# Ten groups of a decoder trunk: the load two weights ahead goes behind the adding transfer, the squares of the next weights behind the keys' last square

## The chip, the core and the metric

The kernel runs on one core of a Trainium2 chip. The metric is the device time of one execution in microseconds (us); three timed runs of the kernel before gave 1653.38, 1652.49 and 1649.63, a median of 1652.49.

## What is computed

Two layers of a decoder trunk over 512 tokens of width 2048. Each normalises its input, projects it with one wide matrix and sends the result through three parallel groups of heads; their outputs, each times a gate, go through an output matrix into the residual stream.

```
def _layer(x, norm_g, w_in, conv_w, ..., w_out):
    h = _rmsnorm(x, norm_g)
    proj = h @ w_in                      # 2048 x 7696
    (cv_h, cv_b, cv_c, cv_g, sb_q, sb_k, sb_v, sb_g,
     gl_q, gl_k, gl_v, gl_g, gl_lr) = split(proj)
    y_conv = short_conv(cv_h, cv_b, cv_c) * silu(cv_g)
    q, k = rmsnorm per head of sb_q, sb_k          # 8 heads of 128
    y_sb = stick_breaking(q, k, sb_v) * silu(sb_g)
    y_gla = rmsnorm(gla(gl_q, gl_k, gl_v, decay(gl_lr))) * silu(gl_g)
    return x + concat(y_conv, y_sb, y_gla) @ w_out
```

The stick-breaking heads need the scores q k of every head, a product of sigmoids along the keys, and that weight times the values. The change concerns the projections of these heads and of the convolution's second half.

## The kernel before, in words

**Groups of weights.** Both matrices are cut into groups of 256 columns, 2048 x 256 numbers of 4 bytes, 2 MB each, listed in the order of use (`specs`). Per layer: six groups of the gated linear attention, four of the convolution's first half, then for each of four pairs of heads (j = 0 to 3) values, gate, queries, keys, which this text calls v j, g j, q j, k j; then conv h 1, conv c 1, conv g 1, conv b 1, and eight groups of the output matrix. TensorE multiplies them one after another.

**A group's way.** `fetch(i)` loads group i into one of only two staging buffers (tile `st`, two transfers of 1 MB on GpSimd's queue, line 360). `squares(i)` lets ScalarE square the group in two halves (tile `junk`, line 379), which gives a bound for its scale. `wscale` sums the bound over the partitions on GpSimd (tile `wgm`, line 395), and a few tiny VectorE operations make the scale (`wq`, `ws`, lines 398 to 413). Then ScalarE rounds the scaled weights to 16 bits (`wh`) and VectorE makes the rest (`wl`): that is the form in which TensorE takes them.

**Quick groups.** Groups g, q, k, conv c 1 and conv g 1 are among those multiplied with seven products in place of eight. They need sums of quarters of the weights. One of these sums is made by an adding transfer: after the first square, GpSimd issues a DMA from `st` into `st` that adds one half of the columns onto the other (tile `st` from `st`, line 382). VectorE makes the others from it (lines 520, 522, 525), and ScalarE and VectorE split each into `wh` and `wl` (lines 500, 501).

**What sets the order.** `weights()` is called when TensorE begins group i. It issues the load of group i + 2 at once and leaves two hooks. The first, called behind the first matmuls of group i, puts down the squares of group i + 1 and its adding transfer; the second puts down its scale and parts. A scheduler then orders each engine's instructions by a simulated time line and by ties such as `order(a, b)`, which only say that a stands behind b in the order and make no engine wait. Each engine, and GpSimd's queue of transfers, takes its instructions in the order so fixed, and waits at one whose data or buffer is not there.

**Around the change.** When TensorE begins v j (j = 1 to 3) or conv h 1, the keys of the pair before have just been multiplied. ScalarE squares them per head into sums (tile `e` from `kT`, eight squares, line 1340), VectorE turns the sums into reciprocal roots (`qrm`, `qr`, `qrt`, lines 1344 and 217 to 222), multiplies the keys by them (line 1357), both engines split the result into two 16-bit parts (`raw`, lines 1361 and 1362), and SyncE issues a DMA transpose of each (line 1366, to tile `kT`; for the queries `qT` from `qp`). The scores (tile `psz`, line 1249) are multiplied behind the values' group and need these transposes. In the same time the parts of the gate's group, or of conv c 1, are made for the group that TensorE takes next.

Of the kernel before, what the change touches and what calls it, by code (L numbers as in the profile page):

```python
# [10 lines left out]
AF = mybir.ActivationFunctionType  # L11
ALU = mybir.AluOpType
# [5 lines left out]
P = 128  # L18
# [25 lines left out]
def hybrid_trunk(ctx, tc, x, norm_g, w_in, conv_w, conv_b, sb_qn_g, sb_kn_g,  # L44
                 gla_w_up, gla_b_up, gla_on_g, w_out, out):
    nc = tc.nc
    V, S, G, T = nc.vector, nc.scalar, nc.gpsimd, nc.tensor
# [4 lines left out]
    HK = KT // 2  # L52
    GW = 256
# [17 lines left out]
    def nm(s):  # L71
        uid[0] += 1
        return f"{s}_{uid[0]}"
# [4 lines left out]
    def wk(shape, tag, bufs=None, dt=F32):  # L78
        return work.tile(shape, dt, tag=tag, name=nm(tag), bufs=bufs)
# [115 lines left out]
    def order(a, b):  # L195
        tc.add_manual_dep(a.ins, b.ins.name, mybir.DependencyInfo(
            mybir.DependencyClass.NoSync, mybir.DependencyReason.DATA), reason="order")
# [116 lines left out]

    quick = set()
    specs = []

    def spec(name, l, src, cols):
        if name in (QUICK[l] if src is w_out else QUICK_IN):
            quick.add(len(specs))  # L320
        specs.append((l, src, cols))

    for l in range(depth):
        for name, cols in (("gla v 0", [(GL_V, GW)]), ("gla v 1", [(GL_V + GW, GW), (GL_LR, LR)]),
# [19 lines left out]
    staged, whole, narrow, peak, scales = {}, {}, {}, {}, {}  # L344
# [3 lines left out]
        return wk([P, HK * GX], "junk", 1, dt=U8)[:, :n]  # L348


    def fetch(i):

        l, src, cols = specs[i]
        queue = nc.gpsimd if i > 2 else nc.sync
        staged[i] = st = []
        whole[i] = stage.tile([P, KT, GW], F32, tag="st", name=nm("st"))
        for h in range(2):
            s_ = whole[i][:, h * HK:(h + 1) * HK, :]
            c0 = cols[0][0]
            queue.dma_start(s_, src[l, h * HK * P:(h + 1) * HK * P, c0:c0 + GW].rearrange("(k p) n -> p k n", p=P),  # L360
                            max_dma_last_dim=1024)
            st.append(s_)
        if len(cols) > 1:
            c0, w = cols[1]
            narrow[i] = wk([P, KT, w], "kT")
            nc.sync.dma_start(narrow[i], src[l, :, c0:c0 + w].rearrange("(k p) n -> p k n", p=P))

    def early(i):
        return i in quick and specs[i][1] is not w_out

    def wmax(i, h):

        if h == 0:
            peak[i] = sm(2 + (i in narrow), "wm")
        if early(i):
            part = whole[i][:, :, (1 - h) * P:(2 - h) * P]
        else:
            part = staged[i][h]
        sq = S.activation(junk(HK * GW).rearrange("p (k n) -> p k n", k=part.shape[1]), part, AF.Square,  # L379
                          accum_out=peak[i][:, h:h + 1])  # L380
        if early(i) and not h:
            G.dma_start(out=whole[i][:, ::2, P:], in_=whole[i][:, ::2, :P], accum_op=ALU.add)  # L382
        if h and i in narrow:
            S.activation(junk(KT * LR).rearrange("p (k n) -> p k n", k=KT), narrow[i], AF.Square,
                         accum_out=peak[i][:, 2:3])
        return sq
# [55 lines left out]
        else:  # L442
            V.tensor_scalar(wh[:, ks, :GW], staged[0][h][:, ks, :GW], scales[0], None, ALU.mult)

    hooks, lastmm = [], [None]

    def whi(i, h):
        wh = wpool.tile([P, HK, GX], F16, tag="wh", name=nm("wh"))
# [13 lines left out]
    def squares(i, mm):  # L462

        with tc.high_priority():
            for h in range(2):
                a = wmax(i, h)
                if not h:
                    order(a, mm)

    def parts_of(i, mm):  # L470

        with tc.high_priority():
            order(wscale(i), mm)
            if i in quick:
                wsums(i)
                return
            for h in range(2):
                whi(i, h)
                wlo(i, h)
# [49 lines left out]
    def weights():  # L529

        i = cursor[0]
        cursor[0] += 1
        if i + 2 < len(specs):
            with tc.high_priority():
                fetch(i + 2)
        assert not hooks
        if i and i + 1 < len(specs):
            hooks.extend([lambda mm: squares(i + 1, mm), lambda mm: parts_of(i + 1, mm)])
        return loaded.pop(i)

    fetch(0)
# [128 lines left out]
    for l in range(depth):  # L670
# [285 lines left out]
        for p in range(2):  # L956
# [3 lines left out]
            a = wk([P, seq], "ga")  # L960
# [26 lines left out]
        for tag in ("qT", "kT"):  # L987
# [10 lines left out]
            s_ = sm(1, "gas")  # L998
# [41 lines left out]
        for p in range(2):  # L1040
# [4 lines left out]
            for li, h in enumerate(LEV[:-1]):  # L1045
                b = li % 2
                e = wk([P, 2, seq // 2], "e")
# [29 lines left out]
            e = wk([P, seq], "e")  # L1077
# [16 lines left out]
            for two, bias in ((0, (nT[:, p, 0:1], None, nT[:, p, 2:3], None)),  # L1094
                              (1, (nT01[:, p:p + 1], nT[:, p, 1:2], None, nT[:, p, 2:3]))):
                e = wk([P, 2, 256], "e")
                n = [0, 0]
# [201 lines left out]
        for j in range(4):  # L1299
            bm = sm(2, "bm")  # L1300
            ps, u = project(False, lambda: wk([P, NT, GW], "kT"))

            vhl = wk([P, 2, NT, GW], "v", dt=F16)
            vh, vl = vhl[:, 0], vhl[:, 1]
            for b in range(2):
                bs = slice(2 * b, 2 * b + 2)
                v3 = ps[b].rearrange("p (a c) -> p a c", a=2)
                S.activation(vh[:, bs, :], v3, AF.Copy, scale=2.0 ** -14)
                V.scalar_tensor_tensor(vl[:, bs, :], v3, 2.0 ** -14, vh[:, bs, :], ALU.mult, ALU.subtract)
            vu = sm(2, "vu")  # L1310
            V.tensor_scalar(vu[:, 0:1], u, 2.0 ** 29, None, ALU.mult)
            V.tensor_scalar(vu[:, 1:2], u, 1.0, None, ALU.mult)
            go()
            g, _ = project_gate(bm[:, 1:2], True)
            m = sm(1, "ggm")
            V.tensor_tensor(m, vu[:, 0:1], bm[:, 1:2], ALU.mult)
            s_ = mixscale(2 + j, m, "b", 12.0)
            go()
            qkT = []
            sq, rm = sm(16, "qs"), sm(16, "qrm")  # L1320
            for n in range(2):
                raw = []

                def dst():
                    raw.append(wk([P, NT, GW], *(("kT",) if n else ("raw", 1))))
                    return raw[0]

                ps, u = project(False, dst)
                copied = bool(raw)
                if not copied:  # L1330
                    raw.append(wk([P, NT, GW], "raw", 1))
                raw = raw[0]
                for b in range(2):
                    rb = raw[:, 2 * b:2 * b + 2, :]
                    if not copied:
                        S.activation(rb, ps[b].rearrange("p (a c) -> p a c", a=2), AF.Copy)
                    e = wk([P, 2 * GW], "e")
                    for i in range(4):
                        cs = slice(i * P, (i + 1) * P)
                        S.activation(e[:, cs], rb.rearrange("p a c -> p (a c)")[:, cs], AF.Square,  # L1340
                                     accum_out=sq[:, 8 * n + 4 * b + i:8 * n + 4 * b + i + 1])
                u2 = sm(1, "gb")
                V.tensor_scalar(u2, u, u, 1.0 / P, ALU.mult, ALU.mult)
                V.tensor_scalar(rm[:, 8 * n:8 * n + 8], sq[:, 8 * n:8 * n + 8], u2, EPS, ALU.mult, ALU.add)
                r8 = raw.rearrange("p a (h c) -> p (a h) c", c=P)
                if not n:
                    qu = sm(1, "qu")
                    V.tensor_scalar(qu, u, nzun[:, l:l + 1], 2.0 ** 25, ALU.mult, ALU.mult)
                    by = kg[:, l, :].rearrange("p (o c) -> p o c", o=1)
                else:  # L1350
                    rs = rsqrt_bits(rm, "q")
                    qz = sm(16, "qz")
                    V.tensor_scalar(qz[:, :8], rs[:, :8], qu, None, ALU.mult)
                    V.tensor_scalar(qz[:, 8:], qz[:, :8], -1.0, None, ALU.mult)
                    V.tensor_scalar(rs[:, 8:], rs[:, 8:], u, None, ALU.mult)
                    by = rs[:, 8:].rearrange("p (a o) -> p a o", o=1)
                V.tensor_tensor(r8, r8, by.to_broadcast([P, 8, P]), ALU.mult)

                top = 2.0 ** 10 if n else 2.0 ** -14
                parts = wk([P, 2, NT * GW], "raw" if n else "qp", 1, F16)  # L1360
                S.activation(parts[:, 0], raw.rearrange("p t c -> p (t c)"), AF.Copy, scale=top)
                V.scalar_tensor_tensor(parts[:, 1], raw.rearrange("p t c -> p (t c)"), top, parts[:, 0],
                                       ALU.mult, ALU.subtract)
                nT_ = wk([P, 2, NT, 2, P], "kT" if n else "qT", dt=F16)
                for i in range(2):
                    nc.sync.dma_start_transpose(nT_[:, i].rearrange("p t h c -> p (t h) c"), parts[:, i])
                qkT.append(nT_)
                go()
            attend(j, *qkT, qz, vh, vl, vu, g, s_)
# [88 lines left out]
```

## Time and profile before

| | |
|---|---|
| timed runs, us | 1649.63, 1652.49, 1653.38 |
| the profiled execution, us | 1652.11 |
| its span in the trace, us | 1650.3 |
| granted TensorE clock, mean | 0.999 |
| TensorE matmul busy, us | 1621.0 |
| VectorE, ScalarE, GpSimd busy, us | 1415.1, 1185.3, 270.0 |

The page and the views of the trace speak of PE (TensorE matmul), PEld (its weight loads), DVE (VectorE), ACT (ScalarE), POOL (GpSimd) and SP (SyncE). L360 is line 360 of the kernel, `st<-in_w_in_dram` is what an instruction writes and reads, and a bracket at a row's end is the engine's idle time before it with what ended that time. A row of a DMA gives the time that its issue took; the time to its landing stands in rows of its own, as lowest, median and highest. Times are from the span's start.

### The profile page before, as it was taken

How to read it: one execution, taken by the hardware profiler on the slowest of the kernel's cores; microseconds unless marked ns; L12 is line 12 of the kernel's file. 1: busy time of each engine (PE TensorE's matmuls, PEld its weight loads, DVE VectorE, ACT ScalarE, POOL GpSimd, SP SyncE). 2: the span in 40 equal slices, each digit the busy share in tenths (PEclk: the TensorE clock that was granted, in tenths of full speed). 3: DMA queues.
4: the chain of work that ended last, by engine and by line, in shares of the span. 5: the costliest groups of instructions: out<-in, count | busy, mean ns of one | idle time of the engine just before them, and what ended most of it. 6: DMA issues, size and time to landing. Idle time of an engine off the chain costs nothing.

```text
span 1650.3 us, 41607 instructions
## 1 busy us (share of the span) xinstructions
PE 1621.0 (98%) x17914; PEld 1341.0 (81%) x17914; DVE 1415.1 (86%) x2377; ACT 1185.3 (72%) x1743; POOL 270.0 (16%) x298
## 2 busy tenths in 40 slices
PE   7999999999999999999999999999999999999999
PEld 5746668988999968789986467689898989668998
DVE  7977989969797979798689689898898989888893
ACT  8667787857777776756765687788786868666571
POOL 0121121111212121111112112112121212111110
PEclk9999999999999999999999999999999999999999
DMA  7144344496767686644543442635777766683441
GB/s 260 58 150 122 70 133 86 111 159 148 167 148 167 148 167 175 170 157 149 193 141 104 115 116 66 178 78 151 148 163 150 161 155 150 158 229 129 154 155 53
DMA packets 193913, 234.90 MB, mean 142 GB/s; under 512 B 90226, under 2 KB 154044, under 8 KB 193216
## 3 DMA queue, kind: packets, MB, share of 16 engines
q0 software_dynamic: 76992, 177.22, 39.9%
q1 hardware_dynamic: 107728, 45.56, 13.7%
q10 hardware_dynamic: 9008, 9.45, 1.8%
q8 instruction: 140, 2.29, 0.6%
q14 instruction: 45, 0.37, 0.1%
HBM read 179.65 MB, written 14.68 MB: 118 GB/s over the span
## 4 chain that ended last, share of the span: by engine, by line
PE 40%; DVE 5%; ACT 3%; DMA 1%; issue 1%; POOL 0%; DVEq 0%; ACTq 0%; POOLq 0%
PE psp L781 11%; PE psp L778 7%; PE psp L828 5%; PE psp L697 3%; PE psp L698 3%; PE psp L699 3%; PE psp L686 3%; PE psp L687 3%; PE psp L688 2%; DVE wl L501 1%; ACT junk L379 1%; ACT wh L500 1%; DVE za L1265 1%; PE psm L1289 1%; DMA st<-in_w_in_dram 1%
## 5 line engine op out<-in xcount | busy, mean ns | idle before, releaser
L500 ACT ACTIVATE wh<-st,ws 128x1024 f16<-128x1024 f32 x252 | 281.7, 1147 | 194.0 <-DVE st L520 96.7
L501 DVE SCALAR_TENSOR_TENSOR wl<-st,ws,wh 128x1024 f16<-128x1024 f32 x252 | 318.0, 1283 | 37.9 <-ACT wh L500 37.8
L379 ACT ACTIVATE junk<-st 128x2048 uint8<-128x2048 f32 x150 | 285.7, 1905 | 16.7 <-DMA st<-in_w_in_dram 8.5
L778 PE MATMUL psp<-s,wh 128*128 128x256 f16 x1152 | 195.6, 273 | 0.0
L778 PEld LDWEIGHTS <-wh 128*128 128x128 f16 x1728 | 168.3, 98 | 22.4 <-issue 2.1
L781 PE MATMUL psp<-wh,s 128*128 128x128 f16 x2048 | 176.7, 219 | 0.0
L697 PE MATMUL psp<-wh,m 128*128 128x256 f16 x640 | 174.5, 273 | 0.0
L698 PE MATMUL psp<-wl,m 128*128 128x256 f16 x640 | 174.5, 273 | 0.0
L699 PE MATMUL psp<-wh,m 128*128 128x256 f16 x640 | 174.5, 273 | 0.0
L781 PE MATMUL psp<-wl,s 128*128 128x128 f16 x1024 | 173.2, 219 | 0.0
L781 PEld LDWEIGHTS <-s 128*128 128x128 f16 x3072 | 172.9, 98 | 0.0
L457 DVE SCALAR_TENSOR_TENSOR wl<-st,ws,wh 128x2048 f16<-128x2048 f32 x68 | 158.9, 2347 | 14.7 <-ACT wh L450 14.7
L450 ACT ACTIVATE wh<-st,ws 128x2048 f16<-128x2048 f32 x66 | 130.7, 1998 | 41.8 <-DVE ws L411 22.8
L360 POOL DMA_DIRECT2D st<-in_w_in_dram x114 | 102.7, 905 | 344.3 <-DVE w7l L501 119.9
L778 PE MATMUL psp<-s,wl 128*128 128x256 f16 x576 | 156.7, 273 | 0.0
L395 POOL PARTITION_ALL_REDUCE wgm<-wm x75 | 54.3, 724 | 489.9 <-ACT junk L379 477.2
L781 PEld LDWEIGHTS <-m 128*128 128x128 f16 x2304 | 131.1, 98 | 2.2 <-issue 1.6
L382 POOL DMA_DIRECT2D st<-st x34 | 53.8, 1584 | 276.5 <-ACT junk L379 236.1
L778 PEld LDWEIGHTS <-wl 128*128 128x128 f16 x864 | 84.5, 98 | 16.0 <-issue 6.0
L781 PE MATMUL psp<-wh,m 128*128 128x128 f16 x1024 | 91.5, 219 | 0.3 <-DVE raw L794 0.3
L781 PE MATMUL psp<-wl,m 128*128 128x128 f16 x512 | 87.5, 219 | 0.0
L688 PEld LDWEIGHTS <-wl 128*128 128x128 f16 x448 | 43.8, 98 | 53.7 <-DVE wl L457 2.3
(442 smaller groups left out, 4203.0 us busy)
## 6 DMA issues: line engine op xcount, KB each, us to landing
st<-in_w_in_dram POOLq DMA_DIRECT2D x114, 1024.0 KB, 8.2
st<-in_w_out_dram POOLq DMA_DIRECT2D x32, 1024.0 KB, 8.4
st<-st POOLq DMA_DIRECT2D x34, 512.0 KB, 7.0
st<-in_w_in_dram SPq DMA_DIRECT2D x6, 1024.0 KB, 11.8
mixd<-g POOLq DMA_DIRECT2D x20, 256.0 KB, 6.9
x<-in_x_dram SPq DMA_DIRECT2D x4, 1024.0 KB, 5.1
qT<-in_x_dram ACTq DMA_DIRECT2D x8, 512.0 KB, 6.2
qT<-xs ACTq DMA_DIRECT2D x8, 512.0 KB, 3.9
```

The lines of the kernel that those rows point to most:

```text
L360: queue.dma_start(s_, src[l, h * HK * P:(h + 1) * HK * P, c0:c0 + GW].rearrange("(k p) n -> p k n", p=P), max_dma_last_dim=1024)
L379: sq = S.activation(junk(HK * GW).rearrange("p (k n) -> p k n", k=part.shape[1]), part, AF.Square, accum_out=peak[i][:, h:h + 1])
L450: hi = S.activation(wh[:, :, :GW], staged[i][h], AF.Copy, scale=scales[i])
L457: V.scalar_tensor_tensor(wl[:, :, :GW], staged[i][h], scales[i], wh[:, :, :GW], ALU.mult, ALU.subtract)
L500: hi = S.activation(h_, b, AF.Copy, scale=sc)
L501: V.scalar_tensor_tensor(l_, b, sc, h_, ALU.mult, ALU.subtract)
L697: T.matmul(o, ah[:, t, k, :], wh[:, kk, :n], start=st_, stop=False, skip_group_check=True)
L698: T.matmul(o, ah[:, t, k, :], wl[:, kk, :n], start=False, stop=False, skip_group_check=True)
L699: return T.matmul(o, al[:, t, k, :], wh[:, kk, :n], start=False, stop=en, skip_group_check=True)
L778: mm = T.matmul(o, w[q_][:, kk, :], a[p_][:, :, kk, :], start=st_, stop=en, skip_group_check=True)
L781: mm = T.matmul(o[:, t * P:(t + 1) * P], a[p_][:, t, kk, :], w[q_][:, kk, :], start=st_, stop=en, skip_group_check=True)
L828: mm = T.matmul(o[:, :n], a_[:, t, k, :], w[k // HK][part][:, k % HK, :n], start=i == 0 and k == 0, stop=i == 2 and k == KT - 1)
```

## The change

In the groups v 0 to v 3 and conv h 1 of both layers ("held", ten in all), `weights()` no longer issues the load of group i + 2. The first hook issues it, after it has put down group i + 1's squares and adding transfer, and with a tie behind that transfer. And the squares of the group that follows such a group (g j, conv c 1) are both tied behind the keys' last square: `ksq` holds it after each pair's keys, and is emptied by the next squares.

```
+    names = []
 ...
+        names.append(str(name))
 ...
-    def fetch(i):
+    def fetch(i, behind=None):
 ...
-            queue.dma_start(s_, src[l, h * HK * P:(h + 1) * HK * P, c0:c0 + GW].rearrange("(k p) n -> p k n", p=P),
-                            max_dma_last_dim=1024)
+            load = queue.dma_start(s_, src[l, h * HK * P:(h + 1) * HK * P, c0:c0 + GW].rearrange(
+                "(k p) n -> p k n", p=P), max_dma_last_dim=1024)
+            if behind is not None:
+                order(load, behind)
 ...
         if early(i) and not h:
-            G.dma_start(out=whole[i][:, ::2, P:], in_=whole[i][:, ::2, :P], accum_op=ALU.add)
+            added[0] = G.dma_start(out=whole[i][:, ::2, P:], in_=whole[i][:, ::2, :P], accum_op=ALU.add)
 ...
-    hooks, lastmm = [], [None]
+    hooks, lastmm, ksq, added = [], [None], [], [None]
 ...
                 a = wmax(i, h)
                 if not h:
                     order(a, mm)
+                if ksq:
+                    order(a, ksq[0])
+            ksq.clear()
 ...
-        if i + 2 < len(specs):
+        held = names[i][:2] == "v " or names[i] == "conv h 1"
+        if i + 2 < len(specs) and not held:
             with tc.high_priority():
                 fetch(i + 2)
         assert not hooks
+
+        def first(mm):
+            squares(i + 1, mm)
+            if held:
+                with tc.high_priority():
+                    fetch(i + 2, added[0])
+
         if i and i + 1 < len(specs):
-            hooks.extend([lambda mm: squares(i + 1, mm), lambda mm: parts_of(i + 1, mm)])
+            hooks.extend([first, lambda mm: parts_of(i + 1, mm)])
 ...
-                        S.activation(e[:, cs], rb.rearrange("p a c -> p (a c)")[:, cs], AF.Square,
-                                     accum_out=sq[:, 8 * n + 4 * b + i:8 * n + 4 * b + i + 1])
+                        a = S.activation(e[:, cs], rb.rearrange("p a c -> p (a c)")[:, cs], AF.Square,
+                                         accum_out=sq[:, 8 * n + 4 * b + i:8 * n + 4 * b + i + 1])
+                ksq[:] = [a] if n else []
```

The lines behind these move by 4 to 16: the load is line 362 in the changed kernel, the first square 383, the adding transfer 386, VectorE's first sum 527, the scores 1264, the keys' squares 1355.

GpSimd's order at v 1 of layer 0, before and in the change. `st_4191` is the buffer of g 1, `st_4599` (before) and `st_4610` (in the change) that of q 1; `wgm` is the sum of a bound over the partitions.

```order
L360 DMA st_4191<-in_w_in_dram 128x8x256 x2
L900 DMA mixd_187<-g_1488 1024x1x128
L360 DMA st_4599<-in_w_in_dram 128x8x256 x2
L382 DMA st_4191<-st_4191 128x8x128
L395 ISA wgm_4659<-wm_4607 128x2
```

```order
L362 DMA st_4191<-in_w_in_dram 128x8x256 x2
L915 DMA mixd_187<-g_1488 1024x1x128
L386 DMA st_4191<-st_4191 128x8x128
L362 DMA st_4610<-in_w_in_dram 128x8x256 x2
L399 ISA wgm_4659<-wm_4604 128x2
```

The load of q 1 and the adding transfer of g 1 have changed places. The same exchange stands at all ten groups.

ScalarE's order at the same place, before and in the change: `e` from `kT` are the keys' squares, `junk` those of g 1's weights, `wh` its first parts.

```order
L1340 ACTIVATE e_4562,qs_3776<-kT_4190 128x128 x2
L379 ACTIVATE junk_4608,wm_4607<-st_4191 128x2048
L1340 ACTIVATE e_4567,qs_3776<-kT_4190 128x128 x2
L1340 ACTIVATE e_4562,qs_3776<-kT_4190 128x128 x2
L1340 ACTIVATE e_4567,qs_3776<-kT_4190 128x128
L379 ACTIVATE junk_4611,wm_4607<-st_4191 128x2048
L1340 ACTIVATE e_4567,qs_3776<-kT_4190 128x128
L500 ACTIVATE wh_4667<-st_4191,ws_4663 128x1024
L1361 ACTIVATE raw_4592<-kT_4190 128x1024
L500 ACTIVATE wh_4669<-st_4191,ws_4663 128x1024
```

```order
L1355 ACTIVATE e_4562,qs_3776<-kT_4190 128x128 x2
L1355 ACTIVATE e_4567,qs_3776<-kT_4190 128x128 x2
L383 ACTIVATE junk_4605,wm_4604<-st_4191 128x2048
L1355 ACTIVATE e_4562,qs_3776<-kT_4190 128x128 x2
L1355 ACTIVATE e_4567,qs_3776<-kT_4190 128x128 x2
L383 ACTIVATE junk_4608,wm_4604<-st_4191 128x2048
L1377 ACTIVATE raw_4592<-kT_4190 128x1024
L507 ACTIVATE wh_4667<-st_4191,ws_4663 128x1024
L507 ACTIVATE wh_4669<-st_4191,ws_4663 128x1024
```

The keys' square that is last in the program stands fourth of the eight in ScalarE's order. The first weight square has moved from behind the second key square to behind the fourth, and the second from before the eighth to behind it; `raw` has moved ahead of the first `wh`. This exchange of the squares is found at v 1 of both layers; at v 2, v 3 and conv h 1 the squares stood so before, and only `raw` and `wh` exchange. On VectorE, at the same groups, the four scale operations and the first `wl` go behind the keys' product (line 1357 before).

## The prediction

> **What bounds the kernel now.** I read the page's engine shares first, then the busy time in stretches of 20 us, then TensorE's own waits, and last each engine in order of time around the one place that these point to.
>
> ```profile
> PE 1621.0 (98%) x17914; PEld 1341.0 (81%) x17914; DVE 1415.1 (86%) x2377; ACT 1185.3 (72%) x1743; POOL 270.0 (16%) x298
> 340.00:360.00 20.00, 17.60 (x159) 15.39 (x158) 8.63 (x23) 7.63 (x19) 2.00 (x2) 1.00 1.23 173
> 360.00:380.00 20.00, 17.25 (x151) 14.51 (x151) 19.16 (x31) 17.26 (x25) 3.84 (x4) 1.00 0.38 56
> 380.00:400.00 20.00, 19.34 (x295) 18.61 (x294) 19.75 (x30) 17.58 (x26) 4.17 (x4) 1.00 0.67 149
> 440.00:460.00 20.00, 20.00 (x180) 17.24 (x178) 16.27 (x25) 16.82 (x24) 2.66 (x2) 1.00 0.32 43
> 1160.00:1180.00 20.00, 20.00 (x183) 17.50 (x181) 18.19 (x26) 13.99 (x20) 1.97 (x2) 1.00 0.85 107
> 1200.00:1220.00 20.00, 19.66 (x342) 19.40 (x339) 19.82 (x36) 15.98 (x25) 2.58 (x3) 1.00 0.83 165
> ```
>
> TensorE is the bound: 1621.0 of 1650.3 us busy. A change that takes away no matmul can only win back its idle time, so the question is how much of that lies where the change acts. After the bounds of each stretch come its length, then busy PE, PEld, DVE, ACT and POOL. In layer 0 around v 1, PE lacks 2.40, 2.75 and 0.66 us in three neighbouring stretches, 5.81 together. The same group of layer 1 (1160 to 1180) lacks nothing, and only 0.34 us some 40 us later; v 2's stretch (440 to 460) lacks nothing. Of the ten groups that the change touches, this one alone has idle PE worth naming.
>
> What PE waited for between 340 and 400:
>
> ```profile
> PE psz L1249 <- DMA kT<-raw: 2.8, 2, 2.3
> PE psp L778 <- DVE g L794: 1.6, 1, 1.6
> PE psp L781 <- ACT wh L500: 0.8, 1, 0.8
> PE psp L781 <- DVE raw L794: 0.7, 1, 0.7
> ```
>
> That is 5.9 us, the same gaps: 2.8 for the transposed keys of pair 0 (the scores, line 1249), then 3.1 in products of g 1 and q 1 whose operands VectorE and ScalarE bring late. Why both are late, engine by engine (of the three rows on landing the first is of the add at 341.14, the second of all 34 adds, the third of the load at 335.25):
>
> ```profile
> 335.25 1.77 POOL L360 DMA_DIRECT2D st<-in_w_in_dram  x2 [3.91 <-DVE wl L457]
> 341.14 1.59 POOL L382 DMA_DIRECT2D st<-st  x1 [4.13 <-ACT junk L379]
> DMA to landing us min/median/max: 17.6/17.6/17.6
> DMA to landing us min/median/max: 6.4/7.0/17.6
> DMA to landing us min/median/max: 15.4/16.5/17.6
> 338.72 1.91 ACT L379 ACTIVATE junk<-st 128x2048 uint8<-128x2048 f32 x1 [3.99 <-DMA st<-in_w_in_dram]
> 340.63 0.30 ACT L1340 ACTIVATE e<-kT 128x128 f32<-128x128 f32 x1
> 343.99 0.30 ACT L1340 ACTIVATE e<-kT 128x128 f32<-128x128 f32 x1
> 344.41 0.27 DVE L1344 TENSOR_SCALAR qrm<-qs,gb 128x8 f32<-128x8 f32 x1 [6.67 <-ACT e L1340]
> 346.45 1.29 DVE L501 SCALAR_TENSOR_TENSOR wl<-st,ws,wh 128x1024 f16<-128x1024 f32 x1
> 348.46 1.23 DVE L1357 TENSOR_TENSOR kT<-kT,qr 128x1024 f32<-128x1024 f32 x1
> 350.81 6.51 SPq L1366 DMA_TRANSPOSE kT<-raw  x2
> 351.95 1.28 DVE L501 SCALAR_TENSOR_TENSOR wl<-st,ws,wh 128x1024 f16<-128x1024 f32 x1
> 358.82 1.23 DVE L520 TENSOR_TENSOR st<-st 128x1024 f32<-128x1024 f32 x1 [5.59 <-DMA st<-st]
> 359.49 0.38 PE L1249 MATMUL psz<-kT,qT 128*128 128x512 f16 x1 [2.26 <-DMA kT<-raw]
> ```
>
> GpSimd issues the load of q 1 at 335.25 and g 1's adding transfer only at 341.14, when ScalarE's first square of g 1 is done. The load's second half lands at 336.14 + 17.6 = 353.7, the add behind it at 341.14 + 17.6 = 358.7, where 34 adds have a median of 7.0. VectorE, free at 353.23, stands 5.59 us for it. Meanwhile ScalarE takes two squares of g 1 between the keys' squares, so that the last of these starts at 343.99 and the chain to the transposes begins at 344.41.
>
> **The change part by part.** *The add ahead of the load.* The add still waits for the first square, which cannot start before g 1 has landed at 338.7, so it is issued at about 341.14 as now. With no load of q 1 ahead of it I take the median, 7.0: landed at 348.1. The bounds are 6.4 and the 10.5 that v 2's add took with a load in front (below): 347.5 to 351.6. All of these are before VectorE can use it (350.4, next part), so the 5.59 us end.
>
> *The squares behind the keys' squares.* Only in v 1 does ScalarE's order change; in the six later groups the first square already stood behind the fourth key square. In v 1 the four key squares behind the first weight square now run together: 340.63 + 4 x 0.29 = 341.8, and the chain starts at about 341.9 instead of 344.41, 2.5 us sooner. The scheduler also puts g 1's scale and its first low part behind the keys' product: 1.2 us (346.45's row up to 347.65) and some 0.5 us of four tiny operations leave the stretch up to 348.46. The product comes 4.2 us sooner, at 344.3, and the first transpose, 350.81 now, at 346.6. If its time to the scores is unchanged, these could start at 359.49 - 4.2 = 355.3, while PE comes to them at 359.49 - 2.26 = 357.23: the 2.8 us go, with 1.9 to spare.
>
> *What VectorE then has.* Keys' low part 346.6 to 347.8, two low parts of 1.28 to 350.4, then line 520: 8.4 us before its present 358.82, and 6.8 before the scores. In v 2 that distance is 7.8 (439.39 to 447.17) without a gap behind it; in layer 1's v 1 it is 4.3 with 0.34 behind it:
>
> ```profile
> 439.39 1.22 DVE L520 TENSOR_TENSOR st<-st 128x1024 f32<-128x1024 f32 x1
> 447.17 1.79 PE L1249 MATMUL psz<-kT,qT 128*128 128x512 f16 x12
> 1167.08 1.23 DVE L520 TENSOR_TENSOR st<-st 128x1024 f32<-128x1024 f32 x1
> 1171.43 1.68 PE L1249 MATMUL psz<-kT,qT 128*128 128x512 f16 x10
> ```
>
> Lying between them nearer v 2, layer 0 should lose the other 3.02 too. Layer 1's 0.34 I leave uncounted; it is the lower bound's.
>
> *What is now late: the load.* In v 1 it starts at 341.14 + 1.59 = 342.7 instead of 335.25 and holds GpSimd until 344.5, so g 1's sum over partitions starts 0.2 us later; it is covered by the keys' product, behind which VectorE now takes the scale. For the six groups v 2, v 3 and conv h 1 of both layers I take v 2:
>
> ```profile
> 424.96 1.77 POOL L360 DMA_DIRECT2D st<-in_w_in_dram  x2 [2.66 <-DVE kT L801]
> 428.27 1.59 POOL L382 DMA_DIRECT2D st<-st  x1 [1.54 <-ACT junk L379]
> DMA to landing us min/median/max: 7.7/8.8/9.8
> DMA to landing us min/median/max: 10.5/10.5/10.5
> 435.57 4.03 SPq L1366 DMA_TRANSPOSE kT<-raw  x2
> DMA to landing us min/median/max: 5.0/5.0/5.0
> 443.44 1.90 ACT L379 ACTIVATE junk<-st 128x2048 uint8<-128x2048 f32 x1
> 447.37 2.19 ACT L500 ACTIVATE wh<-st,ws 128x1024 f16<-128x1024 f32 x2 [1.94 <-PE psp L699]
> ```
>
> (7.7 to 9.8 is the load's landing, 10.5 the add's, 5.0 that of the keys' transpose.) The load moves from 424.96 to 428.27 + 1.59 = 429.86. At 9.8 its second half lands at 440.6; ScalarE's square of it starts at 443.44: cover 2.8 us, and behind the square ScalarE idles another 1.94 until PE frees a buffer. The other bound is v 1's 17.6: 448.4, ScalarE 4.9 late, 3.0 beyond the idle. I take 9.8 and nothing, since pair 1's query transposes, which ran beside the load, will be through by 429.86; what it meets at its tail is the keys' transposes from 435.57, whose landing of 5.0 leaves 447.17 - 440.6 = 6.6 us before the scores. The add landing sooner there gains nothing: line 520 starts at 439.39 behind VectorE's own work, after the add's 438.8. In the two groups v 0 the load goes behind the add too, and GpSimd frees 1.8 us later; q 0's square comes 25 us later:
>
> ```profile
> 245.84 1.67 POOL L382 DMA_DIRECT2D st<-st  x1
> 273.21 1.57 POOL L382 DMA_DIRECT2D st<-st  x1 [8.55 <-ACT junk L379]
> ```
>
> *The sum.* The profiled execution took 1652.11 us, 1.8 more than its span, and lies 0.4 under the median of 1652.49. 1652.11 - 5.81 = 1646.3.
>
> [...]
>
> **The rivals.** *Half the gain (transposes against the load).* In v 1 the keys' transposes from 346.6 meet the load issued at 342.7. When the queries' transposes met a load there, its halves took 15.4 and 17.6 us instead of v 2's 7.7 and 9.8. If the keys' transposes lose those 4 us again, the 2.8 us stay and only the 3.0 go: 1649.1. For it speaks the present collision; against it, that over half of the load's time is over when the transposes start. It decides once they take over 2 us more than now.
>
> *No change (the stall is no constant of the kernel).* The same code in layer 1 shows no such stall, so it may be one execution's accident, or v 1's load, landing at 342.7 + 0.9 + 17.6 = 361.2, may hold ScalarE at q 1's square and hand the gap on. Against it: the three timed runs reach from 1649.63 to 1653.38, none near 1646. Time: 1652.
>
> *Slower (late loads in six groups).* If the moved loads take 17.6 us in v 2, v 3 and conv h 1, ScalarE is 3.0 us late beyond its idle in each. In v 1 a VectorE late by 5.59 cost PE 3.02 later on, 0.54 per us; 6 x 3.0 x 0.54 = 9.7 lost, and with only the 2.8 of v 1 gained, 1659. It outweighs the full 5.81 from 1.8 us beyond the idle, a landing some 17 us after the issue; in v 2 it was 9.8.
>
> *The change does not do what it says.* In GpSimd's order it does, in all ten groups; the squares' tie moves ScalarE in two groups only. With the tie alone working, the kT part, 2.8 us, is the most: this is the first rival's price again.
>
> **How the numbers follow.** Forecast (whole stall gone, 1644.5 to 1648) 0.50; half the gain 0.22; no change 0.18; slower 0.10. A measurement of this kernel can tell about 0.2%, 3.3 us, from nothing. Half the gain lies at that edge: two thirds of it I give to faster, one third to the same. Faster 0.65, same 0.25, slower 0.10. The range reaches from the forecast with layer 1's 0.34 and some 1.5 us of spread up to the no-change case: 1644.5 to 1652.5.
>
> **What would show it.** Right: GpSimd's issue of line 362 behind line 386 in v 1; the add's landing at 7 to 10 us; VectorE's wait at line 527 gone; no wait of PE for kT at line 1264; 20.00 of PE in the stretches from 340 to 400. Wrong: waits of ScalarE at the squares (line 383) for the load in v 2, v 3 or conv h 1, longer than 1.9 us; transposes of the keys that take over 10 us; or idle PE of the old size at a new place between 340 and 420.

## The result, and the profile after

The change makes the kernel faster by 0.4%: 1647.01 us median (1645.30 to 1652.09) against 1652.65 (1647.82 to 1659.48) of the kernel before, timed side by side; the ratio is 0.9964, 95% interval 0.9953 to 0.9976. By the medians that is 5.6 us; the prediction had 1646.3 us and a gain of 5.81.

First the busy time of the changed kernel in the stretches around v 1 of layer 0 (bounds, length, then busy PE, PEld, DVE, ACT and POOL, the granted clock, the DMA share and GB/s):

```profile
340.00:360.00 20.00, 19.52 (x176) 16.77 (x174) 14.02 (x28) 12.53 (x21) 4.28 (x5) 1.00 0.97 166
360.00:380.00 20.00, 20.00 (x184) 17.52 (x182) 19.77 (x30) 14.80 (x23) 3.48 (x4) 1.00 0.67 151
380.00:400.00 20.00, 20.00 (x347) 19.79 (x345) 19.82 (x34) 15.98 (x25) 4.16 (x4) 1.00 0.67 131
```

TensorE lacks 0.48 us where it lacked 5.81. Next the same place by engine, in order of time, with the landing of the add at 341.04 and of the two halves of the load behind it:

```profile
341.04 1.58 POOL L386 DMA_DIRECT2D st<-st  x1 [9.22 <-ACT junk L383]
341.95 2.49 POOL L362 DMA_DIRECT2D st<-in_w_in_dram  x2
DMA to landing us min/median/max: 7.4/7.4/7.4
DMA to landing us min/median/max: 10.5/12.3/14.2
345.14 1.22 DVE L1373 TENSOR_TENSOR kT<-kT,qr 128x1024 f32<-128x1024 f32 x1
347.48 6.24 SPq L1382 DMA_TRANSPOSE kT<-raw  x2
351.14 1.23 DVE L527 TENSOR_TENSOR st<-st 128x1024 f32<-128x1024 f32 x1
358.57 1.57 PE L1264 MATMUL psz<-kT,qT 128*128 128x512 f16 x11 [0.45 <-DMA kT<-raw]
```

The add is ahead of the load and lands in 7.4 us instead of 17.6. VectorE's sum at line 527 (520 before) comes at 351.14 instead of 358.82, with no wait in front. The keys' product and transposes come 3.3 us sooner than before. The scores still wait 0.45 us for the keys.

The profiled execution took 1652.09 us and is the longest of the changed kernel's twenty. Layer 0's gain is in it, but its span of 1650.3 us is that of before: TensorE was busy for 3.0 us more in all (1624.0 against 1621.0), and three stretches of layer 1 lack 3.9 us together:

```profile
1280.00:1300.00 20.00, 19.95 (x344) 19.63 (x342) 19.72 (x35) 14.64 (x22) 2.35 (x3) 1.00 1.02 148
1300.00:1320.00 20.00, 17.35 (x262) 16.59 (x262) 12.61 (x20) 15.38 (x40) 3.78 (x5) 1.00 0.70 156
1480.00:1500.00 20.00, 18.80 (x154) 14.39 (x153) 15.48 (x32) 13.14 (x15) 2.65 (x4) 1.00 0.77 247
PE psp L796 <- issue: 1.9, 1, 1.9
```

The kernel before had 20.00 us of TensorE in all three stretches of its first profile. The 1.9 us at line 796 is time in which TensorE waited for nothing that the profile shows. The edit does not touch these places; a second profile, below, tells whether they belong to the change.

### The profile page after: what moved, and what is told of

Its sections match the earlier page's. It is cut to its first block, busy times and chain, and to the rows that moved or that the text cites. A ratio compares the mean times of both kernels' runs of the same rounds, so it can differ in the third digit from the quotient of the medians.

```text
span 1650.3 us, 41605 instructions
## 1 busy us (share of the span) xinstructions
PE 1624.0 (98%) x17914; PEld 1342.5 (81%) x17914; DVE 1418.1 (86%) x2377; ACT 1184.7 (72%) x1743; POOL 265.8 (16%) x298
## 4 chain that ended last, share of the span: by engine, by line
PE 37%; DVE 6%; DMA 4%; ACT 2%; issue 1%; POOL 0%; SPq 0%; DVEq 0%; ACTq 0%; POOLq 0%
PE psp L796 10%; PE psp L793 6%; PE psp L843 5%; PE psp L712 3%; PE psp L714 3%; PE psp L713 3%; PE psp L701 2%; PE psp L702 2%; PE psp L703 2%; DMA st<-in_w_in_dram 2%; DVE wl L508 1%; DMA m<-mixd 1%; DMA th<-za 1%; DVE za L1280 1%; DMA kT<-raw 1%
## 5 line engine op out<-in xcount | busy, mean ns | idle before, releaser
L461 DVE SCALAR_TENSOR_TENSOR wl<-st,ws,wh 128x2048 f16<-128x2048 f32 x68 | 158.9, 2346 | 14.6 <-ACT wh L454 13.8
L362 POOL DMA_DIRECT2D st<-in_w_in_dram x114 | 109.8, 1029 | 297.8 <-DVE w7l L508 110.7
L793 PEld LDWEIGHTS <-wl 128*128 128x128 f16 x864 | 84.5, 98 | 13.4 <-issue 3.4
```

Of the source, the lines that this page charges most:

```text
L362: load = queue.dma_start(s_, src[l, h * HK * P:(h + 1) * HK * P, c0:c0 + GW].rearrange("(k p) n -> p k n", p=P), max_dma_last_dim=1024)
L461: V.scalar_tensor_tensor(wl[:, :, :GW], staged[i][h], scales[i], wh[:, :, :GW], ALU.mult, ALU.subtract)
L793: mm = T.matmul(o, w[q_][:, kk, :], a[p_][:, :, kk, :], start=st_, stop=en, skip_group_check=True)
```

## The experiments

### The kernel before, once more

No edit.

> The kernel before once more, for a second profiled execution. Theory of the forecast (the stall belongs to the kernel's order): TensorE again lacks about 5.8 us in the three stretches from 340 to 400, with the first adding transfer of g 1 landing near 17 us after its issue and the keys' transposes awaited for about 2 us at line 1249. Rival (the stall is one execution's accident): the three stretches lack under 2 us, the add lands near the 7.0 us of its median, and idle time of that size stands somewhere else or nowhere.

1654.24 us median, ratio of the kernel to itself 1.0002 (0.9983 to 1.002). Its landings (load of q 1, then g 1's add) and its middle stretch:

```profile
DMA to landing us min/median/max: 15.5/16.6/17.7
DMA to landing us min/median/max: 18.1/18.1/18.1
360.00:380.00 20.00, 18.02 (x142) 14.28 (x142) 19.16 (x28) 17.26 (x25) 3.84 (x4) 0.91 0.39 53
```

The stall is there again: 2.49, 1.98 and 0.65 us lack in the three stretches from 340 to 400. The clock of 0.91 (third column from the end) is new and comes up below.

### The changed kernel, once more

No edit.

> The changed kernel once more, for a second profiled execution. If the forecast holds: ratio to before near 0.9964, the stretches from 340 to 400 lack at most 0.5 us, and the 1.9 us that TensorE stood at line 796 near 1302, the 3.0 of conv's pair that followed, and the 1.2 at line 714 near 1488 in the first profile are gone or elsewhere, since no step of the change touches those places; the span is then 1643 to 1646. Rival (the loads issued later cost layer 1 what layer 0 gained): the same stalls stand at the same places again, 5 us together from 1150 to 1550.

1645.86 us, ratio 0.9959 (0.9944 to 0.9974). TensorE has 20.00 us in all three stretches from 340 to 400. The 1.9 us near 1302 and what followed it are gone; of the rest 0.5 us at line 714 are left. So the losses at those three stretches in the first profile are that execution's, not the change's; the kernel before has such losses too, 1.23 us from 1480 to 1500 in b_again and 1.75 from 1300 to 1320 in b_third (below). This profiled execution took 1649.37 us, the longest of its twelve, and its span of 1647.6 misses the 1643 to 1646 that were expected. In layer 1's v 1 a wait for the keys stands in both profiles, 0.9 us in the first and here

```profile
PE psz L1264 <- DMA kT<-raw: 1.3, 1, 1.3
```

where the two profiles of before had 0.3 and 1.5 us of late operands instead. That is no gain and no loss.

### The load alone, the squares alone

Both start from the changed kernel. The first leaves the squares untied, the second leaves every load where it was:

```diff
# load_only
-                ksq[:] = [a] if n else []
+                pass
# squares_only
-        held = names[i][:2] == "v " or names[i] == "conv h 1"
+        held = False
```

> The load moved behind the add in all ten groups, the weights' squares where they were. Theory of the forecast (two causes in a row, each with its own absolute time): the add lands 7 to 10 us after its issue and VectorE's wait at line 527 (5.6 us) goes, so the 3.0 us of late operands go; the keys' last square still ends at about 344.3 and the scores still wait 2.8 us for the keys' transposes. 1649.6, ratio 0.998. Rival (the stall has one cause, the transfers in front of the add): with the load out of the way the transposes land sooner too, all 5.8 us go, ratio 0.9965. Rival (transposes against the load): the transposes issued at 350.8 take longer than 6.5 us and the gain is under 2 us.

> The squares tied behind the keys' last square, the loads where they were. Theory of the forecast: the keys' chain starts 2.5 us sooner and the wait for kT goes (2.8 us), but the add still lands near 358.7, an absolute time, and VectorE stands at line 527 until then; TensorE, 2.8 us sooner at the projections behind the scores, waits there 2.8 us longer for g 1's operands. So nothing is gained, 1652 (ratio 0.9985 to 1.000). If the two parts add up on their own instead: 1649.8, ratio 0.998.

The load alone: 1647.79 us, ratio 0.9972 (0.9953 to 0.9991). The squares alone: 1654.38 us, ratio 1.0003 (0.9986 to 1.002). Of load_only, the keys' transposes, line 527 and the scores:

```profile
351.19 4.53 SPq L1382 DMA_TRANSPOSE kT<-raw  x2
353.66 1.22 DVE L527 TENSOR_TENSOR st<-st 128x1024 f32<-128x1024 f32 x1
358.04 1.57 PE L1264 MATMUL psz<-kT,qT 128*128 128x512 f16 x11 [0.20 <-DMA kT<-raw]
```

Of squares_only the keys' product, their transposes, line 527 and the scores:

```profile
345.79 1.23 DVE L1373 TENSOR_TENSOR kT<-kT,qr 128x1024 f32<-128x1024 f32 x1
348.13 10.76 SPq L1382 DMA_TRANSPOSE kT<-raw  x2
360.12 1.23 DVE L527 TENSOR_TENSOR st<-st 128x1024 f32<-128x1024 f32 x1 [9.55 <-DMA st<-st]
360.77 0.38 PE L1264 MATMUL psz<-kT,qT 128*128 128x512 f16 x1 [2.79 <-DMA kT<-raw]
```

With the squares tied, the product starts 2.7 us and the transposes 2.7 us sooner than before (348.46 and 350.81), and yet the scores wait 2.79 us, to 360.77. With the load moved and the squares as they were, the transposes are issued at 351.19, later than before, and the scores wait 0.20 us. So the wait for the keys did not come from ScalarE's order of squares. It came from the transfers, as did the wait for the add. One cause had two symptoms; a profile of the kernel before without the stall, further below, bears this out. load_only gave more than the 1649.6 of my theory because it had both 2.8 and 3.0 us to give. Its interval holds the 0.998 of that theory as well as the 0.9965 of the rival with one cause; it is the wait of 0.20 in the trace that decides for the rival. The time of squares_only came out as expected, but not in the expected way: the wait for the keys was to go, and it stayed.

### The queries' transposes left out

In the kernel before, one collision partner is taken away; the scores of pair 0 in layer 0 are then zeros:

```diff
+                if l == 0 and j == 0 and n == 0:
+                    order(G.memset(nT_.rearrange("p i t h c -> p (i t h c)"), 0.0), recent[0])
-                for i in range(2):
+                for i in range(2 if l or j or n else 0):
                     nc.sync.dma_start_transpose(nT_[:, i].rearrange("p t h c -> p (t h) c"), parts[:, i])
```

(`recent[0]` is the last load issued.)

> The kernel before, with one thing left out: the two transposes of the queries of pair 0 in layer 0 (issued at 333.25 and 336.11 before); their target is zeroed by GpSimd some 30 us earlier, so the scores of pair 0 there are zeros. Load and add of v 1 stay in their old order. Theory A, formed from the first four runs (one cause: the load of q 1 and the queries' transposes run at the same time and hold each other up from 338 to 346, and the adding transfer and the keys' transposes are late behind them): without the transposes the load's halves land 8 to 10 us after their issue, the add within 11, the keys' transposes by 357, the stretches from 340 to 400 lack under 1 us, and the time is 1647 to 1648.5, ratio 0.9965 to 0.998. Theory B (the add is late because it stands behind a load on GpSimd's own queue, the transposes are innocent): the add lands 16 to 18 us after its issue as before, VectorE stands over 4 us at line 520, and the ratio is 0.999 to 1.000.

1647.65 us, ratio 0.9977 (0.9959 to 0.9995). The load's two halves, the add behind it, and VectorE's sum (line 521 here):

```profile
DMA to landing us min/median/max: 7.7/8.7/9.7
DMA to landing us min/median/max: 7.0/7.0/7.0
355.45 1.23 DVE L521 TENSOR_TENSOR st<-st 128x1024 f32<-128x1024 f32 x1
```

The add stands behind the load in GpSimd's order, as before, and lands in 7.0 us. One profile without the stall could be chance, as the next sections show, but the times agree: two of the twelve took 1650.5 us or more, where of the kernel before it is 102 of 139. Theory B falls: what made load and add late was the queries' transposes running at the same time. In the trace TensorE still lacks 1.62 us from 360 to 400 here, against under 1 us expected: the bound was too tight, the mechanism holds. This profiled execution took 1653.14 us, the longest of its twelve; so a long execution is by itself no sign of the stall.

### Which of the ten groups matter

All three start from the changed kernel:

```diff
# v1_only
+        held = names[i] == "v 1"
# l0_v1_only
+        held = names[i] == "v 1" and not specs[i][0]
# not_v1
+        held = names[i] in ("v 0", "v 2", "v 3", "conv h 1")
```

> The load held behind the add in the two groups v 1 alone, with the squares' tie; the eight other groups as before. The forecast's sum (the moved loads of the other groups cost and gain nothing): as the whole change, 1646 to 1647, ratio 0.996, the stretches from 340 to 400 lack at most 0.5 us. Rival (the late loads of the other groups cost something; they landed 12.1 to 13.6 us after their issue, not the 9.8 of the forecast): faster than the whole change, under 1645, ratio 0.9945 or less. Opposite rival (the adds that land sooner there gain): slower than it, 1648.5 or more.

> The load held behind the add in one group alone, layer 0's v 1; the squares' tie stays in all. If the gain belongs to that one place: as v1_only, 1646 to 1647, ratio 0.996. In layer 1's v 1 the wait of TensorE for the keys' transposes, 0.9 and 1.3 us in the two profiles of the whole change, goes, and the late operands some 20 and 40 us later, 0.3 to 1.5 in the two profiles of before, come back: 0.7 us either way, below what the timing can tell. If half of the gain came from elsewhere: 1649, ratio 0.998.

> The complement: the load held behind the add in v 0, v 2, v 3 and conv h 1, but not in v 1; the squares' tie stays. If the gain belongs to v 1 of layer 0: no gain, 1652 to 1654, ratio 0.999 to 1.001, and the stretches from 340 to 400 lack 5 us or more, as with the squares' tie alone. Rival (late loads cost): slower than before by more than 2 us, ratio 1.0015 or more. Rival (the held loads gain in every group): ratio 0.998 or less.

v1_only 1647.36 us, ratio 0.9987 (0.9961 to 1.0012, wide through two executions of 1661 and 1662 us); l0_v1_only 1647.22, ratio 0.9977 (0.9960 to 0.9994); not_v1 1652.50, ratio 1.0005 (0.9982 to 1.0029). The medians say that layer 0's v 1 has the whole gain. The intervals do not carry that alone: the one of l0_v1_only also holds the 0.998 of half the gain, and the one of v1_only also no gain at all. In the trace of l0_v1_only TensorE has 20.00 us in all three stretches from 340 to 400, the wait for the keys in layer 1 is gone and a late operand is back there, as expected:

```profile
PE psp L796 <- DVE raw L809: 0.6, 1, 0.6
```

The expectation for not_v1 was wrong in one respect. Its median is that of before, but its profiled execution (1646.79 us) shows no stall at all: load and add of v 1, in the old order, landed like this

```profile
DMA to landing us min/median/max: 9.2/10.2/11.3
DMA to landing us min/median/max: 10.7/10.7/10.7
```

and TensorE had 20.00 us in all three stretches. The load is issued 2.00 us after the first of the queries' transposes, as in before. So the old order in v 1 may jam, that is make load, transposes and add late together, in some executions and not in others.

### Does the old order jam every time?

The kernel before a third time, and not_v1 a second time.

> The kernel before a third time. Theory D, from the spread of before's times and from the profile of not_v1 (the old order meets the collision every time, but does not jam every time): profile and time go together. If the load of q 1 lands over 15 us after its issue, the execution takes 1650.5 us or more and lacks 5 us in the stretches from 340 to 400; if it lands within 12 us, it takes under 1648.5 and lacks under 1 us there. Rival (the spread of the times comes from elsewhere): a long landing with a time under 1648.5, or a short one with 1650.5 or more.

> The complement once more (load held in v 0, v 2, v 3 and conv h 1, v 1 in the old order), whose first profile showed no jam: load landed 9.2 and 11.3 us after its issue and 20.00 us of TensorE in all three stretches from 340 to 400, at 1646.79 us. Theory D: profile and time go together as in b_third; from the share of long times so far (8 of its 12 at 1651.6 or more) a jam in this profile is twice as likely as none. Rival (holding the loads of the other groups removes the jam in v 1 too): no jam again, with times of over 1651 all the same.

The old order does not jam every time. b_third's profiled execution took 1647.18 us, the shortest of its eight, with the median of these at 1652.72. not_v1_again's took 1648.20, again without a jam (load 9.3 to 11.6 us, add 11.1, 20.00 in all three stretches); its median is 1650.03, ratio 0.9984 (0.9968 to 1.000). First the kernel before as profiled for the prediction, then b_third, in steps of 2 us; the last column is GB/s, the one ahead of it the share of the DMA engines' time that their packets took:

```profile
338.00:340.00 2.00, 2.00 (x21) 1.80 (x19) 0.00 (x0) 1.28 (x1) 0.00 (x0) 1.00 1.29 66
340.00:342.00 2.00, 2.00 (x21) 1.79 (x20) 0.00 (x0) 2.00 (x12) 0.85 (x1) 1.00 1.87 45
342.00:344.00 2.00, 2.00 (x21) 1.80 (x19) 0.00 (x0) 2.00 (x5) 0.74 (x1) 1.00 0.80 41
344.00:346.00 2.00, 2.00 (x21) 1.79 (x19) 1.48 (x11) 1.11 (x4) 0.40 (x1) 1.00 0.81 80
346.00:348.00 2.00, 2.00 (x20) 1.78 (x19) 1.90 (x6) 0.41 (x1) 0.00 (x0) 1.00 1.25 313
```

```profile
338.00:340.00 2.00, 2.00 (x21) 1.79 (x19) 0.39 (x2) 1.25 (x1) 0.00 (x0) 1.00 1.18 195
340.00:342.00 2.00, 2.00 (x21) 1.78 (x20) 0.00 (x0) 2.00 (x11) 0.83 (x1) 1.00 1.18 343
342.00:344.00 2.00, 2.00 (x21) 1.80 (x19) 0.00 (x0) 2.00 (x4) 0.76 (x1) 1.00 0.93 208
344.00:346.00 2.00, 2.00 (x21) 1.80 (x19) 1.46 (x11) 1.12 (x5) 0.40 (x1) 1.00 1.03 342
DMA to landing us min/median/max: 9.1/10.3/11.4
350.81 3.38 SPq L1366 DMA_TRANSPOSE kT<-raw  x2
353.27 1.23 DVE L520 TENSOR_TENSOR st<-st 128x1024 f32<-128x1024 f32 x1
357.72 1.79 PE L1249 MATMUL psz<-kT,qT 128*128 128x512 f16 x12
```

Before moves 41 to 80 GB/s for 8 us, b_third 195 to 343 in the same 8 us. b_third's load lands in 9.1 and 11.4 us, line 520 does not wait, and TensorE lacks 0.24 us from 340 to 400. Its keys' transposes are issued at 350.81, as in before, and the scores do not wait for them: with ScalarE's order and the issue unchanged, the wait for the keys is gone with the jam. Theory D holds for these profiles: of the six profiles with the old order in v 1 and both partners, three have the jam (before, b_again, squares_only) and took 1652.11, 1654.64 and 1655.59 us; three have none (b_third, not_v1 twice) and took 1647.18, 1646.79 and 1648.20. The times fit it: of the 139 timed executions of the kernel before, 102 took 1650.5 us or more and 13 under 1648; of the changed kernel's 32 it is 1 and 24. The rival of not_v1_again is not ruled out: neither profile of not_v1 shows a jam, and 6 of its 20 times lie under 1648, a larger share than in before. On the other side 11 of the 20 took 1650.5 or more. Whether the loads held elsewhere make the jam in v 1 rarer is open.

### The load after the queries' transposes, still ahead of the add

In the kernel before, GpSimd waits for the queries' transposes by copying from their target (`landed`) into the buffer of the load; the add is tied behind the load, the squares are untied:

```diff
+        if landed is not None:
+            for h in range(2):
+                G.tensor_copy(whole[i][:, h * HK, 0:1], landed[:, 1, NT - 1, 1, P - 1:P])
...
+            if ahead:
+                order(add, ahead.pop())
```

> The kernel before, its old order kept (load of q 1 ahead of the add, squares untied), but in v 1 of layer 0 GpSimd starts the load only when the queries' second transpose has landed (it copies two elements of it into the buffer first). Theory A (only the overlap with the queries' transposes makes the stall): load issued near 342, landed by 356, the add behind it, issued near 344, landed by 356; VectorE at line 520 is late by 0 to 3 us instead of 5.6 and TensorE lacks 0.5 to 2 us from 340 to 400; the time 1647 to 1649.5, ratio 0.997 to 0.9985. Theory C (the add has to be ahead of the load, as the change puts it): the add lands near 359 again and the three stretches lack 3 us or more, ratio 0.9985 to 1.000.

1652.23 us, ratio 1.0005 (0.9990 to 1.002): no gain. The add's issue and landing, VectorE's sum (line 530 here), and TensorE's waits from 340 to 400:

```profile
345.09 1.64 POOL L390 DMA_DIRECT2D st<-st  x1
DMA to landing us min/median/max: 11.5/11.5/11.5
356.67 1.22 DVE L530 TENSOR_TENSOR st<-st 128x1024 f32<-128x1024 f32 x1 [3.38 <-DMA st<-st]
PE psp L788 <- DVE g L804: 1.6, 1, 1.6
PE psp L791 <- ACT wh L510: 1.0, 1, 1.0
PE psz L1259 <- DMA kT<-raw: 0.4, 1, 0.4
```

There is no jam (the load lands in 6.0 and 8.5 us), and the wait for the keys is 0.4. But GpSimd, held until 342.83, issues the add 4 us later than before, it lands at 356.6, and 2.6 us of late operands remain. TensorE lacks 3.04 us from 340 to 400. Theory A had the landing nearly right and its price too low (0.5 to 2 us expected); theory C had the price right and the landing wrong (near 359). So load and transposes kept apart are not enough when the load, put off, puts off the add that stands behind it; in no_q_transposes the add stood behind a load issued early, landed in 7.0 us, and the gain was there. The change keeps the two apart and leaves the add its time. Why its median lies 1.9 us above its profiled execution of 1650.36 is open; part of the price is the clock, in the last section.

## Why the prediction was right, and where it was not

**What bounds, and where.** Right. TensorE's idle time in layer 0's v 1 was what the change could win, and by the medians of l0_v1_only and not_v1 nothing else gained; their intervals leave room for some of it elsewhere.

**The add ahead of the load.** Right in every size: landed in 7.4 us (7.0 forecast), line 527 at 351.14 (350.4), the 5.59 us wait gone.

**The squares behind the keys' squares.** This step failed. Its sizes for VectorE were near (product at 345.14 against 344.3, transposes at 347.48 against 346.6), but "If its time to the scores is unchanged" was not so. In before PE's last wait for these keys ended at 360.39:

```profile
360.39 1.57 PE L1249 MATMUL psz<-kT,qT 128*128 128x512 f16 x11 [0.53 <-DMA kT<-raw]
```

From the issue of the transposes to the end of the last wait for them it was 360.39 - 350.81 = 9.6 us there, 358.57 - 347.48 = 11.1 in the change, and 358.04 - 351.19 = 6.9 in load_only. At 9.6 the keys would have been there at 357.1, before PE came to their second half at 358.12. The transposes now run beside the load, which lands at 342.8 + 14.2 = 357.0. In load_only they start 3.7 us later, 1.5 us before the load's first half lands instead of 5.0, and the scores go on 0.5 us sooner. That is the meeting of the first rival, 1.5 us more than before where that rival decides from 2; in layer 0 it cost 0.45 us and in the second profile nothing, in layer 1 about 1 us. In before, too, the keys' transposes, issued at 350.81, ran beside the load, whose second half was under way until 353.7. The 2.8 us went all the same, but for the 0.45: with the jam gone, the start 3.3 us sooner outweighed the 1.5. In load_only the wait went without the sooner start. The tie has not been shown to be worth anything: the intervals of load_only's 0.9972 and of the whole change's 0.9959, timed with it, overlap.

**The sum.** Right for an execution with a jam: 5.81 forecast, 5.33 by the stretches (59.52 against 54.19). Its two terms were not two. I read the keys' lateness off ScalarE's chain because its times fitted, and took the load's collision as a matter of the add alone; the runs show one collision behind both. That the sum came out all the same is luck in this respect: the change contained the cure of the one cause, the load taken away from the queries' transposes, for another reason.

**The rivals.** *No change (the stall is no constant of the kernel)* was half right, and I gave it too narrow a meaning: the stall is absent from three of six profiles with the old order, but present often enough to set the median. The short profiles of the old order (1646.79 to 1648.20) lie where the changed kernel's times lie. What the change wins is therefore mostly that nearly every execution is now like the good ones: its highest time is 1652.09, that of before 1659.48. *Slower (late loads in six groups)*: the loads were later than I took them, the mechanism did not reach its point. ScalarE's waits for loads at the squares before (all of them, how many, the longest), and then those of the changed kernel behind the landing of its load in v 2 of layer 0, for which I took 9.8 us:

```profile
ACT junk L379 <- DMA st<-in_w_in_dram: 8.5, 5, 4.0
```

```profile
DMA to landing us min/median/max: 10.4/11.6/12.7
ACT junk L383 <- DMA st<-in_w_in_dram: 8.8, 11, 2.0
```

In all six groups the second halves landed 12.5 to 13.6 us after their issue, short of the 17 from which that rival decides. The waits are more in number and shorter, and the total is about the same; the 2.0 is at a load that the change leaves in place, and behind the moved loads of those six groups only one wait stands, 0.42 us in layer 0's conv h 1. v1_only, which leaves these loads early, is no faster by its median.

**Layer 1's v 1**, which I left uncounted, came out at nothing: 0.3 to 1.5 us of late operands turned into 0.9 to 1.3 us of waiting for keys.

**The signs named.** Right: line 362 behind 386, the landing, line 527. Nearly right: 0.48 us lacking instead of none, the wait at line 1264 gone in one profile and 0.45 in the other. Of the signs against, one came true if the time to the last wait is counted, keys' transposes of over 10 us, and pointed at the failed step.

## What to carry to other kernels

When two waits end within a microsecond of each other at one place, ask for the one transfer time behind both before costing them apart: a table of GB/s in steps of 2 us around the place showed a near standstill, 41 to 80 GB/s for 8 us, that no list of waits names. Where a load and a series of transposes meet, try to take the load away from them (load_only: ratio 0.9972), but don't put off a load behind which a transfer stands that is needed soon (load_after_q: 1.0005). And when a stall is a matter of chance, one profile shows whether it happened, not how often: compare the spread of the timed executions too.

## What the runs showed of the hardware

**A load and transposes can bring each other nearly to a standstill.** In the profile of before they moved 41 to 80 GB/s for 8 us (rows above), while the share of the DMA engines' time that packets took stayed at 0.80 to 1.87. In the three profiles with the jam the load's halves landed 15.4 to 18.0 us after their issue, in the three without it 9.1 to 11.6, and with the queries' transposes left out 7.7 and 9.7. The issue of these transposes took 9.73 us in before and 5.07 in b_third. In not_v1 the same two met in the same order, 2.00 us apart as in before, without the jam. What decides is open. The changed kernel's keys, whose transposes met a load early, took 11.1 us from the issue to the end of the last wait; load_only's, issued 3.7 us later, took 6.9. Why the load and the queries' transposes together fell to 58 GB/s on average in before, under a fifth of the 313 that follow, no run here shows.

**TensorE can lose clock behind such waits.** Stretches of 4 us, the clock in the third column from the end, first behind the waits of b_again for the keys (2.96 and 0.51 us), then two stretches of load_after_q, one with no wait and one behind its waits of 0.99 and 1.59:

```profile
360.00:364.00 4.00, 3.02 (x12) 1.47 (x12) 3.97 (x4) 2.81 (x4) 0.00 (x0) 0.67 0.24 52
364.00:368.00 4.00, 4.00 (x36) 3.46 (x35) 3.30 (x5) 4.00 (x5) 1.58 (x1) 0.90 0.00 0
```

```profile
360.00:364.00 4.00, 4.00 (x39) 3.59 (x37) 3.14 (x6) 4.00 (x6) 0.98 (x1) 1.00 0.00 0
376.00:380.00 4.00, 4.00 (x25) 2.99 (x23) 3.97 (x6) 0.00 (x0) 0.49 (x1) 0.60 0.94 273
```

At a clock of 0.60 TensorE did 25 matmuls in 4 us, at 1.00 it did 39 of the same kind: (39 - 25) / 39 x 4 = 1.4 us more, behind a stall of under 3. The profile of before, with waits of 2.26 and 0.53 us and then of 0.76 and 1.60, kept 1.00, and so paid for its jam with the 5.8 us alone. So similar waits were followed by a lower clock in some executions and not in others, and in load_after_q it was waits of no more than 0.99 and 1.59 us, with TensorE at work between them, that 0.60 followed. What decides is open here too. Each clock is a mean over 4 us; no row here shows how it moved within them.

**A TensorE wait with no releaser.** The 1.9 us at line 796 in the changed kernel's first profile, 1.89 in squares_only, 1.74 in l0_v1_only and 1.29 in no_q_transposes stand within 8 us of each other, near 1300, each behind a load there that met transposes and whose second half landed 13.4 to 15.7 us after its issue. In b_third and load_only that load landed after 14.6 and 14.1 us without such a wait. What TensorE stood for there no trace shows, and no run tested it.
